# Attention scores beside the values' column tile, copies by quarters, and one finishing chain for two heads

## The chip, the cores and the metric

The kernel runs on one core of a Trainium2 chip. The metric is the time of one execution in microseconds on the device, and the profile shown below is of one execution on that core. The engines are TensorE (PE: matmuls; PEld: its weight loads), VectorE (DVE), ScalarE (ACT), GpSimd (POOL, here mostly an issuer of DMAs) and SyncE (SP, which issues the weight loads).

## The reference

The reference is one encoder layer over two sequences of 256 tokens with 2048 features, all in float32:

```python
h = h + W_out [ NA(heads 0..7) ; GatedDeltaNet-bidir(heads 0..7) ]( RMSNorm(h) )
h = h + SwiGLU( RMSNorm(h) )
y = RMSNorm(h)
```

`NA` is neighbourhood attention on a grid of 64 columns: per head, scores q k^T plus a position bias, a softmax over the allowed window, and a product with v. `GatedDeltaNet-bidir` runs, for each head, a convolution over q, k and v, and then a recurrence over four chunks of 64 tokens in both directions. Each chunk needs the inverse of a unit triangular 64x64 matrix; there are 128 of them (2 directions, 4 chunks, 8 heads, 2 sequences), one for each partition. The result of a head is normalised by its root mean square and multiplied by a gate silu(z). Both groups go through one output projection, and a feed-forward block follows.

## The kernel before, in words

Every large product is split in three: a float32 operand is written as hi + lo, and `mm3` runs hi*hi, hi*lo and lo*hi. The weights arrive by DMA on SP's queue, ScalarE writes hi (`split`, line 134), VectorE writes lo (line 135), and three buffers of each are in flight. Outputs are made in column tiles of 128 features by 512 tokens (`col_tile`). A column tile is two half tiles (`half_gemm`), each with 24 matmuls of 512 columns.

Small work is put between the matmuls by generators. `half_gemm` calls `pump()` after every second k, so four times in a half tile; I call this a step. `pump` advances the first generator of the queue `chains` and the first of the queue `side`, each to its next `yield`. At the end of a half tile it advances `vector_work` once. `pause(n)` yields n times. So a constant such as `NA_START = 8` says how many steps, each a quarter of a half tile, lie between two pieces of a chain.

TensorE's instructions are pinned to the order of the program: `mm` and `transpose` go through `pin`. On the other engines a planner orders the instructions at compile time by its own estimate of when each is ready. `pin` keeps an instruction behind the one that the program issued before it on the same engine; the copies of `kkq` (line 484) and the first operation of `norms` (line 490) are pinned in that way. Every engine then runs its list strictly in order.

The stages around the change are these. First come the K and Q column tiles of the eight recurrent heads; `kq_post` stores each head's Gram matrices to DRAM (`s_gram`). When the last is stored, the generator `lanes` is put into `vector_work`. It gathers the matrices back with one matrix on each partition (`kkq`, four DMAs by quarters), copies each quarter from the lower to the upper half of the partitions on ScalarE, scales them, solves the triangular systems on VectorE (the loop with `prod` and `W`, lines 557 and 559, 156 instructions of each kind), and stores the result to DRAM (`s_uq`, line 573).

Meanwhile TensorE runs the attention column tiles: for each of eight heads Q, K and V, six half tiles, numbered here from 0 for the first half of head 0's Q. After V, `attend(h)` is put into `chains`. It loads the bias, waits `NA_START` steps, transposes V and makes the scores (lines 605 and 611); the softmax runs on VectorE and ScalarE (lines 619 to 628). `NA_GAP` steps later it transposes the probabilities (line 635), and `PV_GAP` steps later it makes the output product, which `na_o` (line 647) copies and line 648 stores. A head takes 24 steps, so chain and column tiles keep pace.

Then come two column tiles for each recurrent head, its v and its gate z. `prepare` loads the solved matrices (`uq`, line 690, by POOL) and k and q of a head. `recur_pair` runs the four chunks of two heads in step, the first product being `dvn` with `uq` (line 747). `finish_head` squares the output (line 798, written to the tile `yo`, which has one buffer, shared with `pT`), makes a reciprocal square root by Newton steps on VectorE, scales the output `os` (line 806), transposes it (line 812), multiplies by the gate and splits the result into `dmix` (lines 137 and 138). `yo` holds that product too until the split. PSUM has three banks for small products (`sm_tile`) and three for column tiles.

Of the kernel before, what the change touches and what calls it, by code (L numbers as in the profile page):

```python
# [8 lines left out]
F32 = mybir.dt.float32  # L9
# [3 lines left out]
AF = mybir.ActivationFunctionType  # L13
ALU = mybir.AluOpType
# [4 lines left out]
P = 128  # L19
T = 512  # L20
# [3 lines left out]
NB = 2  # L24
# [16 lines left out]


AHEAD = 120
NA_START = 8
NA_GAP = 10
PV_GAP = 5
KQ_START = 20
KQ_GAP = 8
CORE_START = 2
S_GAP = 3  # L50
R_GAP = 2
LANE_START = 4

EARLY = 3
N_GAP = 2
# [10 lines left out]
def r32(ap):  # L66
    return ap.bitcast(F32)
# [3 lines left out]
def hybrid_encoder(ctx: ExitStack, tc: tile.TileContext, xT, w_in, w_ba, w_out, w_gate,  # L71
                   w_up, w_down, w_group, nw_mix, nw_ffn, nw_fin, na_bias, conv_w, lane_par,
                   dn_nw, y):
    nc = tc.nc
    act = nc.scalar.activation
    tt = nc.vector.tensor_tensor
# [5 lines left out]
    def mm(*a, **k):  # L82
        pin(nc.tensor.matmul(*a, **k))  # L83

    def transpose(*a):
        pin(nc.tensor.transpose(*a))
# [16 lines left out]
    ident = cons.tile([P, P], F32, name="ident")  # L103
# [13 lines left out]
    dnw = cons.tile([P, 1], F32, name="dnw")  # L117
# [13 lines left out]
    def split(hi, lo, src, scale=None):  # L131

        if scale is None:
            act(out=hi, in_=src, func=AF.Copy)  # L134
            tt(lo, src, r32(hi), ALU.subtract)  # L135
        else:
            act(out=hi, in_=src, func=AF.Copy, scale=scale)
            stt(lo, src, scale, r32(hi), ALU.mult, ALU.subtract)
# [27 lines left out]
    chains = []  # L166
    side = []
# [24 lines left out]
    def pause(n):  # L192
        for _ in range(n):
            yield
# [11 lines left out]
    def col_tile(src, xs):  # L206
        ps = pg.tile([P, T], F32, tag="g", name="ps_g")
        half_gemm(ps, src[0], xs[:8], True, False)
        half_gemm(ps, src[1], xs[8:], False, True)
        return ps  # L210
# [20 lines left out]
    def sm_tile():  # L231
        return psm.tile([P, T], F32, tag="s", name="ps_s")
# [20 lines left out]
    ps = sm_tile()  # L253
# [46 lines left out]
    def evac(ps, tag, bufs=1, pool=None):  # L300
        t = (pool or wk).tile([P, T], F32, tag=tag, bufs=bufs, name="ev_" + tag)
        pin(tt(t, ps, rstd, ALU.mult))
        return t
# [27 lines left out]
    def ranged(ap, pp):  # L331

        a = ap.rearrange("p (b c t) -> p b c t", b=NB, c=4)
        return a[:, :, 0:4:3] if pp == 0 else a[:, :, 1:3]
# [19 lines left out]
    na = na_cm.__enter__()  # L354
# [40 lines left out]
    rqs = wk.tile([P, 2, 16], F32, tag="rqs", name="rqs")  # L395
# [76 lines left out]
    def lanes():  # L472
# [7 lines left out]
        for d in range(2):  # L480
            nc.gpsimd.dma_start(qq[half[d]], s_qq.rearrange("k h b t -> (k h b) t"))
        yield from pause(LANE_START)
        for sl in quarters:
            pin(nc.scalar.copy(kkq[half[1], sl], kkq[half[0], sl]))
        yield


        def norms(src, nm):
# [41 lines left out]
        ps = sm_tile()  # L530
        mm(ps[:, :P], ones, dg, start=True, stop=True)
        nc.scalar.copy(egl, ps[:, :P])
        ps = sm_tile()
# [5 lines left out]
        for hf in range(2):  # L539
            for pp in range(2):  # L540
                l0 = 3 * P + POS[pp][hf] * 16
# [9 lines left out]
        for c in range(1, C):  # L551
            for s0 in range(0, c, BLK):
# [3 lines left out]
                pv = pr[:, :n * j].rearrange("p (s j) -> p s j", j=j)  # L556
# [20 lines left out]
    for h in range(H):  # L577
# [3 lines left out]
        ps = (ps_k0, ps_k1)[h] if h < 2 else col_tile(w_in[2 * h], xs)  # L581
        conv_silu(ps, 8 + h, kq[:, 0])
        ps = ps_q0 if h == 0 else col_tile(w_in[2 * h + 1], xs)
# [12 lines left out]
        chains.append(kq_post(h, kq, sqh, sql))  # L596


    def attend(h, qT, kT, vT):
        bias = na.tile([P, 2, L], F32, tag="bias", bufs=2, name="bias")  # L600
        nc.gpsimd.dma_start(bias, na_bias[h])
        yield from pause(NA_START)
        pv = sm_tile()
        for i in range(4):
            transpose(pv[:, i * P:i * P + P], vT[:, i * P:i * P + P], ident)
        pq = []
        for b in range(NB):
            ps = sm_tile()
            pq.append(ps)
            for qi in range(2):  # L610
                mm(ps[:, qi * L:qi * L + L], qT[:, b * L + qi * P:b * L + qi * P + P],
                   kT[:, b * L:b * L + L], start=True, stop=True)
        vn = na.tile([P, 4, P], F32, tag="vn", name="vn")
        nc.scalar.copy(vn, pv.rearrange("p (i d) -> p i d", i=4))
        sc = []
        for b in range(NB):
            s = na.tile([P, 2, L], F32, tag=f"s{b}", name="na_s")
            sc.append(s)
            tt(s, pq[b].rearrange("p (q k) -> p q k", q=2), bias, ALU.add)
            mx = na.tile([P, 2], F32, tag="mx", bufs=2, name="mx")  # L620
            nc.vector.tensor_reduce(mx, s, AX.X, ALU.max, negate=True)
            sm = na.tile([P, 2], F32, tag="sm", bufs=2, name="sm")
            for qi in range(2):
                act(out=s[:, qi], in_=s[:, qi], func=AF.Exp, bias=mx[:, qi:qi + 1],
                    accum_out=sm[:, qi:qi + 1])
            nc.vector.reciprocal(sm, sm)
            for qi in range(2):
                act(out=s[:, qi], in_=s[:, qi], func=AF.Copy, scale=sm[:, qi:qi + 1])
        yield from pause(NA_GAP)
        pT = []  # L630
        for b in range(NB):
            pt = sm_tile()
            for kt in range(2):
                for qi in range(2):
                    transpose(pt[:, kt * L + qi * P:kt * L + qi * P + P],
                              sc[b][:, qi, kt * P:kt * P + P], ident)
            t = na.tile([P, 2, L], F32, tag=("pT", "pU")[b], name="pT")
            nc.scalar.copy(t, pt.rearrange("p (q k) -> p q k", q=2))
            pT.append(t)
        yield from pause(PV_GAP)  # L640
        no = na.tile([P, T], F32, tag="s0", name="na_o")
        po = sm_tile()
        for b in range(NB):
            for kt in range(2):
                mm(po[:, b * L:b * L + L], vn[:, b * 2 + kt], pT[b][:, kt],
                   start=(kt == 0), stop=(kt == 1))
        nc.scalar.copy(no, po)
        nc.gpsimd.dma_start(s_na[h], no)

    for h in range(H):  # L650
        ps = col_tile(w_in[16 + 3 * h], xs)
        qT = na.tile([P, T], F32, tag="qT", name="qT")
        pin(stt(qT, ps, QSCALE, rstd, ALU.mult, ALU.mult))
        ps = col_tile(w_in[16 + 3 * h + 1], xs)
        kT = evac(ps, "kT", 1, na)
        ps = col_tile(w_in[16 + 3 * h + 2], xs)
        vT = evac(ps, "vT", 1, na)
        chains.append(attend(h, qT, kT, vT))


    dr_cm = tc.tile_pool(name="dr", bufs=1, side="right", reuse_waits="tile")
# [16 lines left out]
    prepared, outputs, gate, traced, finished = {}, {}, {}, set(), set()  # L678
# [101 lines left out]
    def recur_pair(h):  # L780
        while not {h, h + 1} <= set(prepared):
            yield
        yield from pause(CORE_START)
        yield from together(recur(h), recur(h + 1))
        for i in (h, h + 1):
            side.append(finish_head(i))

    def finish_head(h):
        dr, dmix = state["dr"], state["dmix"]
        while h not in gate:  # L790
            yield
        zs, os_ = gate[h], outputs[h]

        ssq = dr.tile([P, 2, NB], F32, tag="ssq", bufs=2, name="ssq")
        yo = na.tile([P, T], F32, tag="pT", name="yo")
        for pp in (1, 0):
            for b in range(NB):
                act(out=yo[:, :P], in_=os_[:, pp, b], func=AF.Square,
                    scale=rqs[:, pp, h * NB + b:h * NB + b + 1], accum_out=ssq[:, pp, b:b + 1])
        yield  # L800
        rs = dr.tile([P, 2, NB], F32, tag="rs", bufs=2, name="rs_o")
        ts(ssq, ssq, 1.0 / P, EPS, ALU.mult, ALU.add)
        newton_rsqrt(rs, ssq, dr)
        tt(ssq, rs, rqs[:, :, h * NB:h * NB + NB], ALU.mult)
        for pp in (1, 0):
            tt(os_[:, pp], os_[:, pp], ssq[:, pp, :, None].broadcast_to([P, NB, P]), ALU.mult)
        yield from pause(FIN_GAP)
        po = sm_tile()
        po4 = po.rearrange("p (b q t) -> p b q t", b=NB, q=2)
        for pp in range(2):  # L810
            for b in range(NB):
                transpose(po4[:, b, pp], os_[:, pp, b], ident)
        for pp in range(2):
            tt(ranged(yo, pp), po4[:, :, pp].rearrange("p b (c t) -> p b c t", c=2),
               ranged(zs, pp), ALU.mult)
        split(dmix[:, 0, h], dmix[:, 1, h], yo, dnw)
        finished.add(h)

    def start_waiting():
        open_recurrence()  # L820
# [5 lines left out]
    for h in range(0, H, 2):  # L826
        vT = []
        for i in range(2):
# [5 lines left out]
            ps = col_tile(w_in[40 + 2 * (h + i)], xs)  # L834
# [4 lines left out]
        for i in range(h, h + 2):  # L839
            ps = col_tile(w_in[40 + 2 * i + 1], xs)  # L840
            while i > 3 and i - 4 not in finished:
                pump()
            zs = evac(ps, ("vn", "s0", "pU", "zs")[i % 4], 1, state["dr"] if i % 4 == 3 else na)
# [16 lines left out]
    dmix = state["dmix"]  # L860
# [4 lines left out]
    for i in pairs:  # L865
        ps = pg.tile([P, T], F32, tag="g", name="ps_g")
# [7 lines left out]
    for i in pairs[:EARLY]:  # L874
        ps = pg.tile([P, T], F32, tag="g", name="ps_g")
# [30 lines left out]
    for n, i in enumerate(pairs):  # L906
# [3 lines left out]
        else:  # L910
            hk = st.tile([P, T], F32, tag="hk", bufs=2, name="hk")
            nc.sync.dma_start(hk, s_h1[i])
            if n < EARLY:
                ps, wh, wl = early[n]
                mm3(ps, wh[:, 7], wl[:, 7], dns[7][0], dns[7][1], False, True)
            else:
                ps = pg.tile([P, T], F32, tag="g", name="ps_g")
# [418 lines left out]
```

## Time and profile before

| what | value |
|---|---|
| median of 3 runs | 2306.1 us (2305.64 to 2307.92) |
| the profiled execution | 2303.48 us, its span 2301.7 us |
| TensorE busy | 2265.5 us, 98% of the span |
| VectorE busy | 1773.7 us, 77% |
| ScalarE busy | 1067.7 us, 46% |
| mean granted clock of TensorE | 0.994 |

A row of a group or a timeline names the engine, the line of the kernel, the operation, and output and inputs by the program's names, with x for the number of instructions. Many instructions have the line of a helper: 83 is the body of `mm`, 86 that of `transpose`, 134, 135, 137 and 138 those of `split`. The text in brackets is the engine's idle time just before, and what ended it. The times of the timeline are microseconds from the start of the span.

### The profile page before, as it was taken

How to read it: one execution, taken by the hardware profiler on the slowest of the kernel's cores; microseconds unless marked ns; L12 is line 12 of the kernel's file. 1: busy time of each engine (PE TensorE's matmuls, PEld its weight loads, DVE VectorE, ACT ScalarE, POOL GpSimd, SP SyncE). 2: the span in 40 equal slices, each digit the busy share in tenths (PEclk: the TensorE clock that was granted, in tenths of full speed). 3: DMA queues.
4: the chain of work that ended last, by engine and by line, in shares of the span. 5: the costliest groups of instructions: out<-in, count | busy, mean ns of one | idle time of the engine just before them, and what ended most of it. 6: DMA issues, size and time to landing. Idle time of an engine off the chain costs nothing.

```text
span 2301.7 us, 32536 instructions
## 1 busy us (share of the span) xinstructions
PE 2265.5 (98%) x12318; PEld 1928.6 (84%) x12318; DVE 1773.7 (77%) x2740; ACT 1067.7 (46%) x1642; POOL 242.8 (11%) x342
## 2 busy tenths in 40 slices
PE   9999999999999999999999999999999999999998
PEld 6887787888877888788888888888888878888887
DVE  7754699984564645888888888888888778889866
ACT  6777323234332424644444444444444464444435
POOL 2211100002000110100111001101000011011110
PEclk9999999999999999999999999999999999999999
DMA  5333422246331654677777777777776477667772
GB/s 205 126 129 131 122 92 96 97 128 147 102 104 62 215 160 160 207 202 200 211 200 203 195 207 199 207 198 209 196 193 181 153 212 198 176 181 216 183 198 87
DMA packets 112573, 384.74 MB, mean 167 GB/s; under 512 B 14080, under 2 KB 14416, under 8 KB 112160
## 3 DMA queue, kind: packets, MB, share of 16 engines
q1 hardware_dynamic: 77264, 267.17, 33.6%
q0 software_dynamic: 35152, 115.49, 23.7%
q8 instruction: 97, 1.59, 0.3%
q14 instruction: 60, 0.49, 0.1%
HBM read 347.20 MB, written 35.41 MB: 166 GB/s over the span
## 4 chain that ended last, share of the span: by engine, by line
PE 80%; DVE 9%; ACT 5%; issue 3%; DMA 3%; POOL 0%; SPq 0%; DVEq 0%; ACTq 0%; POOLq 0%
PE ps_g L83 25%; PE ps_a L83 14%; PE ps_d L83 14%; PE ps_c L83 14%; PE ps_b L83 7%; PE ps_s L83 5%; DVE w_lo L135 2%; DVE cacc L346 1%; ACT w_hi L134 1%; DVE W L559 1%; DVE prod L557 1%; ACT E L467 1%; PE ps_o L83 1%; DMA w_first<-in_w_group_dram 1%; ACT E L469 1%
## 5 line engine op out<-in xcount | busy, mean ns | idle before, releaser
L83 PE MATMUL ps_g<-xhi,w_hi 128*128 128x512 f32 x896 | 360.9, 403 | 1.9 <-DVE on L437 1.4
L83 PE MATMUL ps_g<-xhi,w_lo 128*128 128x512 f32 x896 | 352.0, 393 | 2.5 <-DVE w_lo L135 2.5
L83 PE MATMUL ps_g<-xlo,w_hi 128*128 128x512 f32 x896 | 351.7, 392 | 0.9 <-DVE xlo L250 0.9
L134 ACT ACTIVATE w_hi<-w_first 128x1024 fp32r<-128x1024 f32 (+1 forms) x180 | 185.7, 1032 | 287.0 <-PE ps_c L83 160.6
L135 DVE TENSOR_TENSOR w_lo<-w_raw,w_hi 128x1024 fp32r<-128x1024 f32 x166 | 202.5, 1221 | 138.5 <-ACT w_hi L134 134.8
L134 ACT ACTIVATE w_hi<-w_raw 128x1024 fp32r<-128x1024 f32 x166 | 174.8, 1055 | 255.9 <-PE ps_g L83 220.8
L134 ACT ACTIVATE w_hi<-b 128x1024 fp32r<-128x1024 f32 (+1 forms) x180 | 185.7, 1031 | 227.3 <-issue 121.9
L135 DVE TENSOR_TENSOR w_lo<-w_first,w_hi 128x1024 fp32r<-128x1024 f32 (+1 forms) x180 | 213.6, 1186 | 52.6 <-ACT w_hi L134 48.1
L135 DVE TENSOR_TENSOR w_lo<-b,w_hi 128x1024 fp32r<-128x1024 f32 (+1 forms) x180 | 212.8, 1182 | 3.0 <-ACT w_hi L134 2.8
L83 PEld LDWEIGHTS ps_g<-xhi,w_lo 128*128 128x128 f32 x896 | 169.5, 189 | 39.9 <-DVE w_lo L135 3.9
L83 PEld LDWEIGHTS ps_g<-xhi,w_hi 128*128 128x128 f32 x896 | 169.8, 189 | 39.6 <-issue 4.4
L83 PEld LDWEIGHTS ps_g<-xlo,w_hi 128*128 128x128 f32 x896 | 169.8, 189 | 36.9 <-DVE xlo L250 2.6
L83 PE MATMUL ps_a<-xc,w_hi 128*128 128x512 f32 x704 | 176.3, 392 | 2.2 <-DVE p L959 2.2
L83 PE MATMUL ps_d<-xc,w_hi 128*128 128x512 f32 x704 | 176.3, 392 | 0.0
L83 PE MATMUL ps_c<-xc,w_hi 128*128 128x512 f32 x704 | 176.3, 392 | 0.0
L83 PEld LDWEIGHTS ps_a<-xc,w_hi 128*128 128x128 f32 x704 | 126.7, 189 | 25.7 <-issue 3.0
L83 PEld LDWEIGHTS ps_d<-xc,w_hi 128*128 128x128 f32 x704 | 126.6, 189 | 22.6
L83 PEld LDWEIGHTS ps_c<-xc,w_hi 128*128 128x128 f32 x704 | 126.6, 189 | 22.6
L134 ACT ACTIVATE w_hi<-w_second 128x1024 fp32r<-128x1024 f32 (+1 forms) x60 | 61.9, 1032 | 92.6 <-PE ps_d L83 84.3
L83 PEld LDWEIGHTS ps_a<-xc,w_lo 128*128 128x128 f32 x704 | 96.0, 190 | 6.9
L83 PEld LDWEIGHTS ps_c<-xc,w_lo 128*128 128x128 f32 x704 | 96.0, 190 | 6.9
L83 PEld LDWEIGHTS ps_d<-xc,w_lo 128*128 128x128 f32 x704 | 96.0, 190 | 6.9
(362 smaller groups left out, 4258.8 us busy)
## 6 DMA issues: line engine op xcount, KB each, us to landing
w_raw<-in_w_in_dram SPq DMA_DIRECT2D x110, 512.0 KB, 3.3
b<-in_w_gate_dram SPq DMA_DIRECT2D x66, 512.0 KB, 3.9
b<-in_w_up_dram SPq DMA_DIRECT2D x66, 512.0 KB, 4.5
b<-in_w_group_dram SPq DMA_DIRECT2D x48, 448.0 KB, 4.1
w_raw<-in_w_out_dram SPq DMA_DIRECT2D x32, 512.0 KB, 3.5
w_raw<-in_w_down_dram SPq DMA_DIRECT2D x24, 512.0 KB, 3.7
w_second<-in_w_gate_dram SPq DMA_DIRECT2D x22, 512.0 KB, 5.7
w_first<-in_w_gate_dram SPq DMA_DIRECT2D x22, 512.0 KB, 5.0
```

What stands on the lines that cost most here:

```text
L83: pin(nc.tensor.matmul(*a, **k))
L134: act(out=hi, in_=src, func=AF.Copy)
L135: tt(lo, src, r32(hi), ALU.subtract)
L346: stt(a3[:, :, lo:hi], x3[:, :, lo + o:hi + o], cw[:, ct, j:j + 1], a3[:, :, lo:hi], ALU.mult, ALU.add)
L467: pin(act(out=E[half[0], s, s:], in_=G[half[0], s:], func=AF.Exp, bias=NG[half[0], s:s + 1]))
L469: pin(act(out=E[half[1], s, :s + 1], in_=G[half[1], :s + 1], func=AF.Exp, bias=NG[half[1], s:s + 1]))
L557: tt(pv, W[:, s0:s1, s0:c], kkq[:, c, 0, None, s0:c].broadcast_to([P, n, j]), ALU.mult)
L559: nc.vector.tensor_reduce(W[:, s0:s1, c], pv, AX.X, ALU.add)
```

## The change

There are three parts.

1. `attend` gets V in a list that is filled later. It is put into `chains` after K's column tile, so that its first steps lie beside V's column tile. The scores come `NA_START = 5` steps after that (formerly 8 steps after V). The transposes of V and the copy `vn` move from ahead of the scores to just ahead of the transposes of the probabilities, `NA_GAP = 13` steps (formerly 10) behind the scores. A loop yields there until V is in the list.
2. In `lanes` the `yield` moves into the loop over the quarters, so one copy is issued at the end of each of four half tiles instead of four at the end of one, and `LANE_START` goes from 4 to 6. All that follows in `lanes` is issued five half tiles later in the program.
3. `finish_pair` takes the place of two `finish_head`, one behind the other. It squares the outputs of both heads, runs the Newton steps once on a tile of twice the size, scales both, and `FIN_GAP` steps later transposes both into two PSUM banks, multiplies and splits them one after the other. The wait for the gate moves from its start to ahead of the transposes.

```diff
-NA_START = 8
-NA_GAP = 10
+NA_START = 5
+NA_GAP = 13
...
-LANE_START = 4
+LANE_START = 6
...
         for sl in quarters:
             pin(nc.scalar.copy(kkq[half[1], sl], kkq[half[0], sl]))
-        yield
+            yield
...
-    def attend(h, qT, kT, vT):
+    def attend(h, qT, kT, v):
         bias = na.tile([P, 2, L], F32, tag="bias", bufs=2, name="bias")
         nc.gpsimd.dma_start(bias, na_bias[h])
         yield from pause(NA_START)
-        pv = sm_tile()
-        for i in range(4):
-            transpose(pv[:, i * P:i * P + P], vT[:, i * P:i * P + P], ident)
...
-        vn = na.tile([P, 4, P], F32, tag="vn", name="vn")
-        nc.scalar.copy(vn, pv.rearrange("p (i d) -> p i d", i=4))
...
         yield from pause(NA_GAP)
+        while not v:
+            yield
+        pv = sm_tile()
+        for i in range(4):
+            transpose(pv[:, i * P:i * P + P], v[0][:, i * P:i * P + P], ident)
+        vn = na.tile([P, 4, P], F32, tag="vn", name="vn")
+        nc.scalar.copy(vn, pv.rearrange("p (i d) -> p i d", i=4))
...
         kT = evac(ps, "kT", 1, na)
+        v = []
+        chains.append(attend(h, qT, kT, v))
         ps = col_tile(w_in[16 + 3 * h + 2], xs)
-        vT = evac(ps, "vT", 1, na)
-        chains.append(attend(h, qT, kT, vT))
+        v.append(evac(ps, "vT", 1, na))
...
-        for i in (h, h + 1):
-            side.append(finish_head(i))
+        side.append(finish_pair(h))
+
+    def finish_pair(h):
+        dr, dmix = state["dr"], state["dmix"]
+        ssq = dr.tile([P, 2, 2, NB], F32, tag="ssq", bufs=2, name="ssq")
+        yo = na.tile([P, T], F32, tag="pT", name="yo")
+        for i in range(2):
+            for pp in (1, 0):
+                for b in range(NB):
+                    l0 = (h + i) * NB + b
+                    act(out=yo[:, :P], in_=outputs[h + i][:, pp, b], func=AF.Square,
+                        scale=rqs[:, pp, l0:l0 + 1], accum_out=ssq[:, i, pp, b:b + 1])
         yield
+        rs = dr.tile([P, 2, 2, NB], F32, tag="rs", bufs=2, name="rs_o")
         ts(ssq, ssq, 1.0 / P, EPS, ALU.mult, ALU.add)
         newton_rsqrt(rs, ssq, dr)
+        tt(ssq, rs, rqs[:, :, h * NB:(h + 2) * NB].rearrange("p q (i b) -> p i q b", i=2),
+           ALU.mult)
+        for i in range(2):
+            for pp in (1, 0):
+                os_ = outputs[h + i]
+                tt(os_[:, pp], os_[:, pp], ssq[:, i, pp, :, None].broadcast_to([P, NB, P]),
+                   ALU.mult)
         yield from pause(FIN_GAP)
+        while h + 1 not in gate:
+            yield
+        pos = []
+        for i in range(2):
+            po = sm_tile().rearrange("p (b q t) -> p b q t", b=NB, q=2)
+            for pp in range(2):
+                for b in range(NB):
+                    transpose(po[:, b, pp], outputs[h + i][:, pp, b], ident)
+            pos.append(po)
+        for i in range(2):
+            if i:
+                yo = na.tile([P, T], F32, tag="pT", name="yo")
+            for pp in range(2):
+                tt(ranged(yo, pp), pos[i][:, :, pp].rearrange("p b (c t) -> p b c t", c=2),
+                   ranged(gate[h + i], pp), ALU.mult)
+            split(dmix[:, 0, h + i], dmix[:, 1, h + i], yo, dnw)
+            finished.add(h + i)
```

More of the change, by code (lines that the diff above doesn't have):

```diff
@@ L784, in recur_pair @@
         yield from together(recur(h), recur(h + 1))
-        for i in (h, h + 1):
-            side.append(finish_head(i))
-    def finish_head(h):
+        side.append(finish_pair(h))
+    def finish_pair(h):
         dr, dmix = state["dr"], state["dmix"]
[L790 to L794, printed above, removed]
+        ssq = dr.tile([P, 2, 2, NB], F32, tag="ssq", bufs=2, name="ssq")
         yo = na.tile([P, T], F32, tag="pT", name="yo")
[L796 to L799, printed above, removed]
+        for i in range(2):
[4 more added lines that the diff above has]
+                        scale=rqs[:, pp, l0:l0 + 1], accum_out=ssq[:, i, pp, b:b + 1])
@@ L800, in finish_head @@
         yield
-        rs = dr.tile([P, 2, NB], F32, tag="rs", bufs=2, name="rs_o")
+        rs = dr.tile([P, 2, 2, NB], F32, tag="rs", bufs=2, name="rs_o")
         ts(ssq, ssq, 1.0 / P, EPS, ALU.mult, ALU.add)
         newton_rsqrt(rs, ssq, dr)
-        tt(ssq, rs, rqs[:, :, h * NB:h * NB + NB], ALU.mult)
-        for pp in (1, 0):
-            tt(os_[:, pp], os_[:, pp], ssq[:, pp, :, None].broadcast_to([P, NB, P]), ALU.mult)
-        yield from pause(FIN_GAP)
-        po = sm_tile()
-        po4 = po.rearrange("p (b q t) -> p b q t", b=NB, q=2)
@@ L810, in finish_head @@
[L810 to L817, printed above, removed]
+        tt(ssq, rs, rqs[:, :, h * NB:(h + 2) * NB].rearrange("p q (i b) -> p i q b", i=2),
[5 more added lines that the diff above has]
+                   ALU.mult)
```

## The prediction

> **What bounds the kernel now.** I read the page first, then the waits of TensorE, then the timelines of the engines named there.
>
> ```profile
> span 2301.7 us, 32536 instructions
> ...
> PE 2265.5 (98%) x12318; PEld 1928.6 (84%) x12318; DVE 1773.7 (77%) x2740; ACT 1067.7 (46%) x1642; POOL 242.8 (11%) x342
> ```
>
> TensorE is busy for 2265.5 of 2301.7 us, and the change gives it the same matmuls and transposes as before. It can win only what TensorE idles, and what idling does to its clock. So the waits of PE are the view that matters (columns: total us, times, longest):
>
> ```profile
> PE ps_s L86 <- DVE os L806: 4.4, 2, 3.8
> ...
> PE ps_s L86 <- ACT na_s L628: 3.7, 3, 1.6
> PE ps_g L83 <- DVE w_lo L135: 3.3, 3, 2.0
> ...
> PE ps_g L83 <- ACT w_hi L134: 0.4, 1, 0.4
> ```
>
> Each is next to one part of the change: the finish of a head (L806), the softmax ahead of the transposes of the scores (L628), and the split of a weight tile (L134, L135). For the last, the timelines of ScalarE and of VectorE:
>
> ```profile
> 238.78 1.91 ACT L484 COPY kkq<-kkq 64x2048 f32<-64x2048 f32 x1 [9.71 <-DMA kkq<-s_gram]
> ...
> 243.81 1.06 ACT L134 ACTIVATE w_hi<-w_raw 128x1024 fp32r<-128x1024 f32 x1
> ...
> 248.53 1.90 ACT L484 COPY kkq<-kkq 64x2048 f32<-64x2048 f32 x1 [0.99 <-DMA kkq<-s_gram]
> ```
>
> ```profile
> 244.90 1.23 DVE L135 TENSOR_TENSOR w_lo<-w_raw,w_hi 128x1024 fp32r<-128x1024 f32 x1 [10.13 <-ACT w_hi L134]
> ...
> 250.46 0.22 DVE L490 TENSOR_SCALAR nkx<-kkq 128x64 f32<-128x64 f32 x1 [3.73 <-ACT kkq L484]
> ...
> 282.46 0.15 DVE L557 TENSOR_TENSOR prod<-W,kkq 128x1 f32<-128x1 f32 x1
> ```
>
> ScalarE stands in order behind copies whose data are still landing (9.71 us), the weight split at 243.81 stands behind two of them, and VectorE loses 10.13 and 3.73 us. VectorE has no time to lose, since it then runs the triangular solve (L557, L559) beside everything else:
>
> ```profile
> 253.90:257.40 3.50, 3.10 (x9) 2.57 (x10) 3.50 (x4) 0.14 (x1) 0.00 (x0) 0.51 0.46 150
> 315.40:318.80 3.40, 3.40 (x13) 2.91 (x12) 3.40 (x8) 2.66 (x12) 0.00 (x0) 0.50 0.44 154
> 356.30:359.80 3.50, 3.50 (x11) 2.85 (x12) 3.50 (x6) 2.36 (x4) 0.00 (x0) 0.51 0.38 138
> 690.80:697.70 6.90, 5.37 (x15) 4.43 (x16) 3.35 (x9) 1.35 (x2) 0.00 (x0) 0.51 0.10 39
> 420.00:460.00 40.00, 40.00 (x185) 33.31 (x184) 40.00 (x64) 12.30 (x22) 1.08 (x2) 1.00 0.26 93
> ```
>
> These are stretches with length, then PE, PEld, DVE, ACT and POOL busy, then the granted clock. From 420 to 460 us VectorE is busy for 40.00 of 40.00 us. The first four rows are the second price of the stalls: beside them the clock fell to 0.51, so 17.3 us ran at half speed.
>
> **Part 1, scores and copies: what goes.** The output copy of each attention head, one per 24 steps (a step is a quarter of a half tile), gives the pace:
>
> ```profile
> 283.73 0.59 ACT L647 COPY na_o<-ps_s 128x512 f32<-128x512 f32 x1 [0.91 <-PE ps_s L83]
> ...
> 325.65 0.59 ACT L647 COPY na_o<-ps_s 128x512 f32<-128x512 f32 x1 [0.91 <-PE ps_s L83]
> ...
> 366.97 0.59 ACT L647 COPY na_o<-ps_s 128x512 f32<-128x512 f32 x1 [0.91 <-PE ps_s L83]
> ...
> 404.51 0.59 ACT L647 COPY na_o<-ps_s 128x512 f32<-128x512 f32 x1 [0.90 <-PE ps_s L83]
> ```
>
> The heads take 41.9, 41.3 and 37.5 us; the last is undisturbed, 1.56 us a step. Two heads are 8.2 us too long, of which I leave 1 us to the transposes of the lanes, which come once: 7.2.
>
> ```profile
> 896.71 0.50 PE L83 MATMUL ps_g<-dmix,w_lo 128*128 128x512 f32 x1 [0.79 <-DVE w_lo L135]
> ```
>
> Before the first copy lie 3.3 + 0.4 us of weight waits, less 0.8 that belongs to a much later stage (this row), one softmax wait of about 1.1, and half of 3.5 us of low clock less 0.4 counted already: 5.3. Together 12.5 us.
>
> The new code spreads the four copies over four half tiles, starting two later: by a count of steps they stand behind the splits of half tiles 8 to 11, when the data have landed. Then neither ScalarE nor VectorE blocks, and the gap of 13 steps instead of 10 gives the softmax 4.7 us more, three times its longest wait. I take all 12.5; the bounds are 7.4 (3.7 + 3.7, the idle alone) and 13.7.
>
> On the clock the Trainium skill (TensorE: Matmul & The Clock Gate, "HAM oscillation") says that idle gaps above about 3.4 us make it fall. The trace differs: the longest softmax wait is 1.6 us, and the clock fell beside two of three. By that rule only the idle goes, the finish below would give 2.7 us less, and the sum would be 2.7 us higher. I take the trace.
>
> **Part 1, what it moves.** The evacuation of K is followed by the scores 6 steps (9.4 us) later, formerly 17. The bias load and the store of the head before keep their order on POOL's queue. The wait for the values' tile adds nothing: it is written 8 steps after the chain starts and read 18 steps after. Transposes of V keep their number and only change place. All this I cost at nothing, because TensorE has column tiles in between; without that cover the evacuation of K is the risk (a rival below).
>
> What is not free is the solve. The fourth copy now stands in program order behind the softmax of head 1, which is issued in the sixth step of its V tile. Before, the end of that tile was at 281.8 us (2 us ahead of the copy at 283.73). Two steps earlier, less 5.3 of stalls, plus 1.9 for the output product now ahead: about 275.5. The scores take 2; the softmax its length in this trace:
>
> ```profile
> 267.23 0.67 DVE L619 TENSOR_TENSOR na_s<-ps_s,bias 128x512 f32<-128x512 f32 x1
> ```
>
> ```profile
> 273.64 0.91 ACT L628 ACTIVATE na_s<-na_s,sm 128x256 f32<-128x256 f32 x2 [0.73 <-DVE sm L626]
> ```
>
> That is 7.3, less 1 that overlaps the scores, and a copy is 1.9: the copies end at 284 to 286 instead of 250.4. From there to the solve it took 32.0 us of VectorE (250.46 to 282.46). Half of that needs only the first three copies and can run ahead, so I take 16: the solve starts near 301, 18 us later. The bounds are 286 (all ahead) and 317 (nothing ahead). It ends later by as much, since VectorE has no gap to catch up in, and a little more because it now shares with more attention work: 20 us.
>
> **Part 1, who waits for that.** The solve's result goes through DRAM to the recurrence:
>
> ```profile
> 493.75 2.28 DVE L567 TENSOR_TENSOR kkq<-W,rb 64x2048 f32<-64x2048 f32 x1
> ...
> 497.80 3.85 DVE L569 TENSOR_TENSOR kkq<-W,nks 64x2048 f32<-64x2048 f32 x1
> ```
>
> ```profile
> 496.33 1.56 POOL L573 DMA_DIRECT2D s_uq<-kkq  x2 [15.33 <-DVE kkq L567]
> 501.95 0.77 POOL L573 DMA_DIRECT2D s_uq<-kkq  x1 [4.06 <-DVE kkq L569]
> 518.05 0.57 POOL L648 DMA_DIRECT2D s_na<-na_o  x1 [15.33 <-ACT na_o L647]
> ...
> 544.87 4.73 POOL L690 DMA_DIRECT2D uq<-s_uq  x7 [16.17 <-DMA s_uq<-kkq]
> ```
>
> ```profile
> 560.06 1.05 PE L83 MATMUL ps_s<-dvn,uq 128*128 128x128 f32 x8
> ```
>
> ```profile
> DMA to landing us min/median/max: 2.9/4.3/17.0
> ```
>
> The last load is issued at 549.6 and lands 4.3 later, at 553.9; the first product needs it at 560.1. So there are 6 us in hand. The change spends them three times. TensorE comes 12.5 us sooner. The recurrence itself is placed three steps sooner (4.7 us): the attention chain of head 7 now ends a column tile earlier and the new pair is first in the queue. So the need is at 560.1 - 12.5 - 4.7 = 542.9. The data come 20 us later, less what POOL's queue gives back: it stood 15.33 us behind the store of head 6, which is a column tile earlier now. The stores still land one after the other, so I take 11 of it: 553.9 + 20 - 11 = 563. The bounds are 547 (solve not moved, 7 given back) and 574 (nothing given back).
>
> TensorE then waits 563 - 542.9 = 20.1 us with the whole program queued behind the product, since its order is fixed. After such an idle the clock is low. At 690.8 a 3.78 us idle left 5.4 us of half speed behind it, worth 2.7; I take 2.6.
>
> **Part 2, the finish in pairs.**
>
> ```profile
> 685.17 0.40 ACT L798 ACTIVATE yo<-os,rqs 128x128 f32<-128x128 f32 x1 [0.82 <-DVE dmix L138]
> ```
>
> ```profile
> 692.33 1.09 PE L86 MATMUL ps_s<-ident,os 128*128 128x128 f32 x4 [3.78 <-DVE os L806]
> ...
> 834.94 0.63 PE L86 MATMUL ps_s<-ident,os 128*128 128x128 f32 x4 [0.64 <-DVE os L806]
> ```
>
> The squares of a second head waited until the first head's result had left the shared buffer yo (L138); the transposes then came too soon. One chain takes the squares of both at once, so 3.78 + 0.64 and the 2.7 of low clock go: 7.1 us. The four squares (0.40 each) and two scalings (0.4) added to each chain lie ahead of transposes 6 steps away, and these steps are short where no recurrence runs beside them. I put 1 us for new waits, bounds 0 and 4. The thirteen small VectorE operations saved per pair save nothing here: no PE wait stands behind them any more. The wait for the gate never holds, since the gates are written at least five half tiles sooner.
>
> **Sum, on the profiled execution.** -12.5 + 20.1 + 2.6 - 7.1 + 1.0 = +4.1 us. That execution took 2303.5 us (span 2301.7 and 1.8 around it), 2.6 under the median of the runs, 2306.1. I carry the difference to the median and round up, as more of the unknown bounds point up: 2311.
>
> **Rivals.**
>
> The data are there in time. If the work ahead of the solve fits before the last copy, or the planner sets the copies sooner, the loads land by 547: 16 us less than the forecast, 2294 or so, and at best, with no wait at all, -12.5 - 7.1 = 2286. It decides from a solve that starts before about 285. For it: VectorE would not lose 13.9 us in front of the solve. Against it: the copy is kept behind the softmax by the program order. Chance 0.28.
>
> K comes too late. With the scores 6 steps behind K, an evacuation more than 9.4 us late stops TensorE. The last matmuls of K, and its evacuation, for heads 1 and 4:
>
> ```profile
> 268.25 0.39 PE L83 MATMUL ps_g<-xhi,w_lo 128*128 128x512 f32 x1
> ...
> 390.54 0.39 PE L83 MATMUL ps_g<-xhi,w_lo 128*128 128x512 f32 x1
> ```
>
> ```profile
> 279.81 0.69 DVE L302 TENSOR_TENSOR ev_kT<-ps_g,rstd 128x512 f32<-128x512 f32 x1
> ...
> 395.65 0.67 DVE L302 TENSOR_TENSOR ev_kT<-ps_g,rstd 128x512 f32<-128x512 f32 x1
> ```
>
> The lag is 11 us in the disturbed head and 5 in the other. If it persists: some 3 us and a clock drop of 1.7 in each of three heads; much of it would shorten the wait at the recurrence. Or the finish holds two of three PSUM banks while the next pair steps: up to 4 a pair. Either adds 8 to 15 us: 2319 to 2326. Chance 0.14.
>
> The copies do not move because the planner, not the yields, sets the order: then the 12.5 stay, the recurrence needs its data at 555 when they land at 554, and the finish gives 7: 2300. Chance 0.06.
>
> The clock rule of the Trainium skill above would give 2314; it lies inside the forecast.
>
> **Numbers.** Forecast (the wait at the recurrence eats the gain, -2 to +14): chance 0.52, of which 0.20 within 0.2% and 0.32 slower. About 0.2%, 4.6 us, is what a measurement of this kernel can tell from no change. Faster: 0.28 + 0.04 = 0.32; same 0.20 + 0.02 = 0.22; slower 0.32 + 0.14 = 0.46. The range 2290 to 2322 leaves out the best of the first rival and the worst of the second.
>
> **What would show it.** Right: no copy of kkq with a DMA wait, no PE wait on na_s or os above 0.5 us, head copies 37.5 us apart from the start, the first L557 near 300, and one PE wait of 10 to 25 us on uq near 545. Wrong: the first product of the recurrence without a wait (the faster rival), or PE waiting for ev_kT (the slower).

## The result, and the profile after

The changed kernel is slower: 2322.6 us (median of 6 runs, 2321.2 to 2323.5) against 2305.3 us for the kernel before beside it (6 runs, 2302.4 to 2307.9). The ratio is 1.0075, with a 95% interval of 1.0062 to 1.0088, so the loss is 17.3 us. The forecast, 2311 us, was 11.6 us too low, and the range ended at 2322, just short of it.

The page of the changed kernel, its span and its first row of busy times:

```profile
span 2321.2 us, 32510 instructions
...
PE 2265.6 (98%) x12318; PEld 1930.8 (83%) x12318; DVE 1762.3 (76%) x2688; ACT 1065.8 (46%) x1640; POOL 242.7 (10%) x342
```

TensorE is busy as long as before (2265.6 against 2265.5 us). Its idle time, span less busy, grew from 36.2 to 55.6 us. That is 19.4 of the 19.5 us between the two spans, so in the net the loss is idle time, and the waits of PE must show it (total us, times, longest):

```profile
PE ps_s L83 <- DMA uq<-s_uq: 21.9, 4, 20.1
PE ps_s L86 <- ACT dvT L350: 9.4, 3, 8.2
PE ps_c L83 <- ACT w_hi L134: 5.2, 2, 3.2
...
PE ps_g L83 <- DVE w_lo L135: 0.8, 1, 0.8
...
PE ps_s L86 <- DVE os L811: 0.3, 1, 0.3
```

The two rows on top are new. Before, `uq` cost no wait in the list and `dvT` 0.7 us. The waits that the change was to remove are gone: none on `na_s`, 0.3 us on `os` (4.4 before), 0.8 us on `w_lo` (3.3 before). The net of the listed rows is 21.9 + 8.7 + 1.1 - 3.7 - 4.1 - 2.5 = +21.4 us; the other listed rows bring it to 19.9, and idle that the view does not list to 19.4.

The timeline of PE has the two long waits, each in the bracket at the end of its row:

```profile
543.41 1.21 PE L86 MATMUL ps_s<-ident,dvT 128*128 128x128 f32 x4 [8.22 <-ACT dvT L350]
...
571.41 0.77 PE L83 MATMUL ps_s<-dvn,uq 128*128 128x128 f32 x2 [20.10 <-DMA uq<-s_uq]
```

The first is the transposes of a recurrent head's V, the second the first product of the recurrence. To see why both came late, follow the solve backwards. These are the copies on ScalarE, and then VectorE from the fourth copy to the end of the solve:

```profile
252.14 1.91 ACT L484 COPY kkq<-kkq 64x2048 f32<-64x2048 f32 x1
...
257.40 1.90 ACT L484 COPY kkq<-kkq 64x2048 f32<-64x2048 f32 x1
...
265.88 1.90 ACT L484 COPY kkq<-kkq 64x2048 f32<-64x2048 f32 x1
...
281.37 1.90 ACT L484 COPY kkq<-kkq 64x2048 f32<-64x2048 f32 x1
```

```profile
283.31 0.22 DVE L490 TENSOR_SCALAR nkx<-kkq 128x64 f32<-128x64 f32 x1 [2.32 <-ACT kkq L484]
283.77 2.28 DVE L517 TENSOR_TENSOR kkq<-kkq,E 128x2048 f32<-128x2048 f32 x1
...
312.34 0.16 DVE L557 TENSOR_TENSOR prod<-W,kkq 128x1 f32<-128x1 f32 x1
...
532.91 3.72 DVE L569 TENSOR_TENSOR kkq<-W,nks 64x2048 f32<-64x2048 f32 x1
536.67 1.23 DVE L135 TENSOR_TENSOR w_lo<-w_raw,w_hi 128x1024 fp32r<-128x1024 f32 x1
537.81 0.68 DVE L302 TENSOR_TENSOR ev_xi<-ps_g,rstd 128x512 f32<-128x512 f32 x1
```

No copy waits for a DMA any more (the longest such wait before was 9.71 us), and VectorE waits 2.32 us for the last copy where it lost 10.13 and 3.73 us. But the fourth copy ends at 283.3 (250.4 before), and not one scaling of `kkq` lies ahead of it: the first, line 517, is at 283.77, behind the read of the diagonal, line 490. The solve starts at 312.3 (282.5 before) and its last operation ends at 536.6 (501.7 before). Behind it in VectorE's order stands the evacuation `ev_xi` of a column tile whose last matmul ended at 527.1. From it come `dvT` on ScalarE (542.94) and the 8.22 us of TensorE.

The result then goes through DRAM, on POOL's queue:

```profile
533.17 1.56 POOL L573 DMA_DIRECT2D s_uq<-kkq  x2 [40.49 <-DVE kkq L567]
...
543.01 0.57 POOL L651 DMA_DIRECT2D s_na<-na_o  x1
...
568.31 4.73 POOL L694 DMA_DIRECT2D uq<-s_uq  x7 [8.89 <-DMA s_uq<-kkq]
```

The stores land one after the other from 541.2 to 567.7, and the loads from 568.7 to 575.4.

### The profile page after: what moved, and what is told of

Read it like the earlier page. It is cut to its first block, busy times and chain, and to the rows that moved or that the text cites. A ratio compares the mean times of both kernels' runs of the same rounds, so it can differ in the third digit from the quotient of the medians.

```text
span 2321.2 us, 32510 instructions
## 1 busy us (share of the span) xinstructions
PE 2265.6 (98%) x12318; PEld 1930.8 (83%) x12318; DVE 1762.3 (76%) x2688; ACT 1065.8 (46%) x1640; POOL 242.7 (10%) x342
## 4 chain that ended last, share of the span: by engine, by line
PE 78%; DVE 12%; ACT 4%; issue 3%; DMA 3%; POOL 0%; SPq 0%; DVEq 0%; ACTq 0%; POOLq 0%
PE ps_g L83 23%; PE ps_a L83 14%; PE ps_c L83 14%; PE ps_d L83 14%; PE ps_b L83 7%; PE ps_s L83 5%; DVE w_lo L135 3%; DVE prod L557 3%; DVE W L559 2%; DVE cacc L346 1%; DMA s_uq<-kkq 1%; ACT w_hi L134 1%; PE ps_o L83 1%; ACT E L467 1%; ACT E L469 1%
```

## The experiments

Three kernels make one part of the change each, beside runs of the kernel before at 2304.7 us. First the copies by quarters alone:

```diff
-LANE_START = 4
+LANE_START = 6
...
-        yield
+            yield
```

> The kernel before with part 2 alone (LANE_START 6, a yield behind each of the four copies). Theory A, the copies carry the loss: the solve starts about 30 us later than in the kernel before (282.5), near 312; the loads of uq land near 573 and the first product of the recurrence, due near 553, waits some 15 to 20 us; slower than before by 6 to 14 us. Rival B, the earlier place of the recurrence (attention chain a column tile sooner) carries it: here the recurrence keeps its place, so no wait on uq above 6 us, and the kernel is faster by 5 us or more because the weight splits are no longer blocked. Rival C, the pairs carry it: as B.

Measured: 2312.4 us, ratio 1.0030 (1.0020 to 1.0040), 7.7 us slower. Its waits of PE:

```profile
PE ps_s L86 <- ACT na_s L628: 6.8, 2, 5.8
...
PE ps_s L86 <- DVE os L806: 4.4, 2, 3.8
PE ps_s L83 <- DMA uq<-s_uq: 4.3, 4, 2.5
```

The solve starts at 308.9, and the last load of `uq` lands at 566.0 instead of 554.1. Yet the wait on it is only 4.3 us, where theory A had 15 to 20: TensorE is ready for the transposes of the last attention head 14.5 us sooner than before (530.5 against 545.0), but waits 5.8 us there for the softmax, behind the late solve, and with further waits and the low clock behind them it asks for `uq` at 559.5, as late as the kernel before (560.1). So the late solve alone costs something, but not what it costs in the whole change.

Then the attention scores alone:

```diff
-NA_START = 8
-NA_GAP = 10
+NA_START = 5
+NA_GAP = 13
...
+        chains.append(attend(h, qT, kT, v))
         ps = col_tile(w_in[16 + 3 * h + 2], xs)
```

> The kernel before with part 1 alone (the attention chain starts beside V's column tile, V is transposed late). Theory A: the solve starts near 282 as before; the recurrence comes three steps sooner, but the store of head 6 no longer stands in POOL's queue, so its loads land near 545 and no wait on uq exceeds 4 us; the softmax waits (3.7 us) go, the blocked weight split stays; between 6 us faster and the same. Rival B: the wait on uq is there (8 us or more) and the kernel is slower by 5 us or more. Another possibility: PE waits for the evacuation of K, 3 us in each of heads 1 to 3.

Measured: 2302.9 us, 0.9991 (0.9982 to 1.0001). The softmax waits are gone, but `uq` is waited for, 3.4 us, the longest 2.3. The solve starts at 279.2.

And the finish in pairs alone:

```diff
-        for i in (h, h + 1):
-            side.append(finish_head(i))
+        side.append(finish_pair(h))
```

> The kernel before with part 3 alone (finish_pair). Theory A: the wait of 3.8 us on os at head 3, its low clock (2.7 us) and the 0.6 us wait at head 7 go, new waits are under 1 us; faster by 4 to 7 us. Rival C, the pairs carry the loss (two of three PSUM banks held, yo handed on within the chain): PE waits of 2 us or more per pair, slower by 3 us or more.

Measured: 2299.0 us, 0.9975 (0.9966 to 0.9985), 5.7 us faster. No wait on `os` of 0.2 us or more is left. This part does about what it was costed at (7.1 less 1.0).

The three effects add up to 7.7 - 1.8 - 5.7 = +0.2 us; together the parts cost 17.3. So the loss lies in how they meet, and the next kernel takes out the part that is late, and keeps the other two:

```diff
-LANE_START = 6
+LANE_START = 4
...
-            yield
+        yield
```

> The changed kernel with part 2 undone (LANE_START 4, all four copies at the end of one half tile). Theory A: ScalarE blocks on the gather again and the weight split waits as before, but the solve starts near 282, the loads of uq land by 548, the wait on uq is under 6 us: faster than before by 6 to 14 us. Rival B: the wait on uq stays above 12 us and the kernel stays slower than before by 8 us or more.

Measured: 2297.9 us, 0.9970 (0.9958 to 0.9982). Two of its waits:

```profile
PE ps_s L83 <- DMA uq<-s_uq: 2.9, 2, 2.4
...
PE ps_s L86 <- ACT dvT L350: 1.1, 2, 0.6
```

Both new waits of the changed kernel have nearly gone, with the solve at 278.3 and the last load landed at 552.2. On top of parts 1 and 3, the copies by quarters cost 1.0075 - 0.9970 of 2305 us, 24 us.

Is it the lateness that costs, or the moving of the copies itself? One kernel keeps the quarters and starts them four half tiles sooner; another keeps the lateness and lets the recurrence ask 12 steps later.

```diff
-LANE_START = 6
+LANE_START = 2
```

> The changed kernel with LANE_START 2 instead of 6, the yields between the copies kept: the copies now stand behind half tiles 4 to 7. Theory A (what costs is how late the last copy stands in the order, not that the copies are spread): the solve starts near 280, the loads of uq land by 554, the wait on uq is under 5 us; faster than before by 6 to 12 us. Rival D (the spreading itself, one copy between the weight splits of each half tile, costs): a wait on uq of 10 us or more stays, slower than before.

Measured: 2305.8 us, 1.0005 (0.9996 to 1.0014). Its waits:

```profile
PE ps_s L86 <- DVE na_s L615: 5.2, 1, 5.2
...
PE ps_s L83 <- DVE ev_kT L302: 2.6, 1, 2.6
PE ps_s L83 <- DMA uq<-s_uq: 2.5, 2, 1.9
```

The solve starts at 286.2 and the wait on `uq` is down from 21.9 to 2.5 us. So the lateness carried that wait. But the 6 to 12 us of theory A did not come, the time is that of the kernel before, and the gain is smaller than that of the kernel with the copies as before: VectorE now scales beside the second head's K, whose evacuation stands behind the scaling of 275.13 (line 525), and TensorE waits for it at 277.67. The 5.2 us come at 327.07, where transposes wait until VectorE has read the scores (line 615). The former is the rival "K too late" of the prediction, at one head and behind the scaling. These waits are not the whole difference: of the 9.1 us between the spans of the two kernels (2304.8 and 2295.7) 3.2 are idle and 5.9 busy time, and this execution has 13.6 us of half speed from 977 us on, in stages without copies, where the other has none before the end of the program.

```diff
-CORE_START = 2
+CORE_START = 14
```

> The changed kernel with CORE_START 14 instead of 2, so the recurrence of each pair is issued 12 steps (some 16 us of column tiles) later. Theory A: the solve and the loads keep their times (312, 575), the wait on uq falls from 20 us to 8 or less, the low clock behind it shrinks, the wait of 8 us on the transposes of V stays; 10 to 18 us faster than the changed kernel, so within 8 us of before. Rival E (the recurrences are the path that sets the end, so what is moved comes back as a wait in the finish of the last pairs): less than 5 us faster than the changed kernel.

Measured: 2306.1 us, 1.0005 (0.9996 to 1.0015), 16 us less than the changed kernel.

```profile
PE ps_s L83 <- DMA uq<-s_uq: 9.8, 4, 8.0
PE ps_s L86 <- ACT dvT L350: 8.3, 1, 8.3
```

The solve is as late as in the changed kernel (313.0), the data even land later (579.7), and nearly all of the loss is gone: twelve more steps of column tiles now lie ahead of the need. So it is the meeting of late data with an early need that costs, and the two waits are of different kinds: the one on `uq` shrank by 12 us, the one on `dvT`, which lies ahead of the recurrence, stayed.

Next the step of the prediction that said that half of the scaling could run ahead of the fourth copy. The diagonal (line 490) is read by quarters, each behind its copy:

```diff
         for sl in quarters:
             pin(nc.scalar.copy(kkq[half[1], sl], kkq[half[0], sl]))
+            pin(ts(nkx[:, sl], dgk[:, sl], EPS, None, ALU.add))
             yield
```

> The changed kernel, in which the diagonal of the gathered matrices is read by quarters, each right behind its copy, instead of once behind the last. If the read of the diagonal keeps back all scaling of the gathered matrices (lines 517 to 527) until the fourth copy has landed, then three quarters of it now run ahead, the solve starts near 300 instead of 312, the loads of uq land 8 to 12 us earlier (565) and the kernel is faster than the changed one by 8 to 12 us. If the scaling is held by something else (the planner's order, the copies themselves), the solve stays within 3 us of 312 and the time within 4 us.

Measured: 2317.0 us, 1.0052 (1.0037 to 1.0067), 5.5 us less than the changed kernel by the medians, short of the 8 to 12 expected, and the ends of the intervals overlap. The trace is of the fastest of its four runs (2312.4 us). VectorE, where lines 487, 522, 530 and 562 answer to 490, 517, 525 and 557, and two waits of PE:

```profile
254.97 1.55 DVE L530 TENSOR_TENSOR kkq<-kkq,E 64x768 f32<-64x768 f32 x1
...
269.12 2.28 DVE L522 TENSOR_TENSOR kkq<-kkq,E 128x2048 f32<-128x2048 f32 x1
...
283.92 0.17 DVE L487 TENSOR_SCALAR nkx<-kkq 128x16 f32<-128x16 f32 x1 [2.91 <-ACT kkq L486]
...
304.97 0.16 DVE L562 TENSOR_TENSOR prod<-W,kkq 128x1 f32<-128x1 f32 x1
```

```profile
PE ps_s L83 <- DMA uq<-s_uq: 20.2, 4, 18.1
...
PE ps_s L86 <- ACT dvT L350: 3.3, 3, 2.1
```

Now the first scaling, 254.97, runs 29 us ahead of the end of the fourth copy (283.9), and the first of line 522 (269.12) 15 us ahead; the solve starts 7.4 us sooner, and the last load lands 8.8 us sooner (566.6). So the whole-tile read of the diagonal did hold them back. It is not all: 16 us were counted, and 21 us still lie between the last copy and the solve. The scalings that now run ahead take 7.6 us together. Behind the fourth copy stay those that need its quarter, the Newton steps, which are made once from the whole diagonal, and the four products with `ndm` (line 532), which need their result. The wait on `dvT` shrinks with the solve's end (6 us), and that on `uq` only by 1.7 in total, since the need came sooner by nearly as much as the data.

The last three kernels look for a better version: the early copies with the recurrence at its old place, three steps later (the scores' earlier chain had moved it three sooner); the same with the copies as before; and the diagonal by quarters with a middle start.

```diff
-CORE_START = 2
+CORE_START = 5
...
-LANE_START = 6
+LANE_START = 2
```

> The changed kernel with LANE_START 2 and CORE_START 5: the copies as early as in the run with LANE_START 2, and the recurrence three steps (4 us) later, where it was in the kernel before. Theory A: no wait on uq, none on the weight splits, none on the softmax; 10 to 16 us faster than the kernel before. Rival: a wait remains, no better than LANE_START 2 alone.

Measured: 2296.7 us, 0.9970 (0.9959 to 0.9982), 9 us less than with the early copies alone, and 8 us less than the kernel before, short of the 10 to 16 expected. No wait on `uq` is listed, but 5.6 us on `na_s` (line 615) and 3.2 us on `ev_kT` remain.

```diff
-CORE_START = 2
+CORE_START = 5
...
-LANE_START = 6
+LANE_START = 4
...
-            yield
+        yield
```

> Parts 1 and 3 with the copies as before (all four at once, LANE_START 4), and CORE_START 5. In the run of parts 1 and 3 alone the wait on uq was 2.9 us, with 6.8 us of low clock beside it. Theory A: three steps more (4 us) take both away; 4 to 6 us faster than parts 1 and 3 alone, so 10 to 13 us faster than before. Rival: the wait moves to the transposes of V or the finish, within 2 us of parts 1 and 3 alone.

Measured: 2290.0 us beside 2306.5 before, 0.9929 (0.9915 to 0.9942). It is the fastest of all, 16 us ahead of the kernel before. From its page, and its first product of the recurrence:

```profile
span 2288.4 us, 32509 instructions
...
PE 2257.7 (99%) x12318; PEld 1924.5 (84%) x12318; DVE 1764.6 (77%) x2688; ACT 1064.0 (46%) x1640; POOL 242.0 (11%) x342
```

```profile
552.53 1.05 PE L83 MATMUL ps_s<-dvn,uq 128*128 128x128 f32 x8
```

The product has no wait in its bracket, and its last load landed at 551.7. Against the same kernel without the three steps the median is 7.9 us lower, more than the wait of 2.9 us that went: the idle fell by 2.1 us (32.8 to 30.7) and the busy time by 5.2 (2262.9 to 2257.7), with the mean granted clock at 0.998 instead of 0.995. Ahead of the end of the program the kernel without the three steps ran 3.4 us from 294.9 and 6.8 us from 550.9, beside the wait on `uq`, at half speed, the one with them only 3.4 us from 1864.5. This is one profiled execution of each.

```diff
-CORE_START = 2
+CORE_START = 5
...
-LANE_START = 6
+LANE_START = 3
...
             pin(nc.scalar.copy(kkq[half[1], sl], kkq[half[0], sl]))
+            pin(ts(nkx[:, sl], dgk[:, sl], EPS, None, ALU.add))
             yield
```

> The changed kernel with the diagonal read by quarters, LANE_START 3 and CORE_START 5: copies behind half tiles 5 to 8, scaling spread behind each copy. Theory A: no blocked weight split, no heap of VectorE work in front of head 1's softmax as with LANE_START 2, solve from 275 to 285, no wait on uq; 12 to 16 us faster than before. If the heap comes back (a wait of 5 us on na_s or ev_kT in heads 1 and 2), 6 to 9 us faster.

Measured: 2292.9 us, 0.9946 (0.9933 to 0.9958). The interval overlaps that of the fastest, so which of the two is better stays open. The solve starts at 287.7, later than the 275 to 285 expected, and one wait of 3.9 us stands at 536.04, on the copy of the last head's probabilities; the trace is of the slowest of the five runs. What matters to both is that the data are there before they are asked for.

## Why the prediction was wrong

The sign of the sum and the place of its largest term were right, and the size was not: +4.1 us were worked out, and the spans of the two profiled executions differ by 19.5 (the medians by 17.3). Two steps failed: that half of the scaling could run ahead of the fourth copy, and that column tiles would cover every other evacuation, for which the sum had nothing. Behind the second lie 11.5 of the 15.4 us that the sum missed, and the first made it worse.

**Stalls ahead of the recurrence, -12.5: held.** The copies of the heads' outputs come at an even pace:

```profile
265.27 0.59 ACT L650 COPY na_o<-ps_s 128x512 f32<-128x512 f32 x1 [0.91 <-PE ps_s L83]
...
302.81 0.59 ACT L650 COPY na_o<-ps_s 128x512 f32<-128x512 f32 x1 [0.91 <-PE ps_s L83]
...
378.60 0.59 ACT L650 COPY na_o<-ps_s 128x512 f32<-128x512 f32 x1 [0.91 <-PE ps_s L83]
```

The first three distances sum to 113.3 us instead of 120.8, a gain of 7.5 where 7.2 was counted. TensorE begins half tile 52, the last to start ahead of the wait on `dvT`, at 528.4 instead of 540.9 us, 12.5 sooner, and by then it has made the last head's transposes and product too, which before came behind this point (about 2.4 us). The gain is nearer 15.

**The finish, -7.1 + 1.0: held.** The kernel with the pairs alone gains 5.7 us, and in the changed kernel the only wait on `os` is 0.3 us.

**"Half of that ... can run ahead": this step failed.** The solve was put at 301, with 317 as the bound for nothing ahead, and it started at 312.3. The copies ended where they were put (283.3, forecast 284 to 286). The read of the diagonal needs all four quarters, and the scalings of lines 525 to 527 write over what it reads, so each had to follow it. Line 517 writes the other half of the tile and yet came behind it too; whether the whole tile is guarded there or the planner chose this order, no run separates. The diagonal by quarters shows the effect: with that read split, both kinds run ahead, 7.6 us of work, and 7.4 us come back, less than half of the 16 that were counted. I had looked at which quarters the scaling needs, and not at which reads must be done before it may write.

From there the data were late by 35.0 us at the solve's end (536.6 against 501.7), where 20 was counted: 29.9 in the start and 5.1 in a longer solve. The queue gave back 13.7 (52.5 us from the solve's end to the last load before, 38.8 after) instead of 11. So the last load landed at 575.4, not 563.

**The wait on `uq`, 20.1: right by two errors.** It measured 20.10 us. The data came 12.4 us later than forecast, but the product starts when the second of the eight loads is in, at 571.3, and not the last. And the need, forecast for 542.9, came at 551.3 (571.4 less 20.1), because the wait on `dvT` stood ahead of it. That the two cancel is luck.

**The wait on `dvT`: not in the sum at all, and the largest term missed.** "TensorE has column tiles in between" was said of the attention's evacuations. The same VectorE has to evacuate the recurrent heads' V, and its order places that behind the solve's last three long operations. A solve that ends late there takes TensorE with it: 8.22 us, 8.7 more than before in all. The kernel with the diagonal by quarters, whose solve ends 9.9 us sooner (526.7), brings the longest down to 2.1, and the one with the copies as before to 0.6.

**The low clock, +2.6 after the wait, was too small.** The stretches at half speed: length, then PE, PEld, DVE, ACT and POOL busy, then the granted clock:

```profile
543.40:549.00 5.60, 5.59 (x17) 4.69 (x18) 2.01 (x4) 0.85 (x2) 3.82 (x5) 0.50 0.98 191
571.40:579.80 8.40, 6.55 (x17) 4.99 (x18) 0.88 (x2) 1.96 (x4) 1.65 (x3) 0.50 0.26 70
996.20:999.60 3.40, 3.40 (x14) 3.01 (x13) 0.13 (x1) 1.26 (x2) 0.00 (x0) 0.50 0.92 330
1897.30:1900.70 3.40, 2.84 (x7) 2.26 (x8) 1.09 (x1) 1.30 (x2) 0.62 (x1) 0.50 1.09 216
```

Half of the busy time in each is lost: 2.8 + 3.3 + 1.7 + 1.4 = 9.2 us. (One more at the end of each program, with PE busy for 1.19 us in it, is the same in both.) The second row is the term that was costed at 2.6. The first belongs to the wait that was not forecast. The last two lie behind waits of 2.16 and 3.16 us in late stages that the change does not touch. With the same working the four stretches shown of before cost 7.7, so the changed kernel spent nearly as much time at half speed as the one before, in other places, and busy time hardly moved.

**The account.** Forecast +4.1; to it 8.7 of idle on `dvT` and 2.8 of slow clock behind it; 0.7 more of slow clock and 1.8 of smaller waits on `uq`; 3.1 of slow clock and 1.1 of wait (`ps_c`) in the late stages; 2.4 more gain ahead of the recurrence and 0.7 fewer waits in the finish. That gives 4.1 + 11.5 + 2.5 + 4.2 - 3.1 = 19.2 of the 19.5 us. The wait on `uq` itself needs no correction, since its two errors cancel. The 4.2 us of the late stages belong to this execution; nothing here ties them to the change.

On the rule that I weighed, the Trainium skill (TensorE: Matmul & The Clock Gate, "HAM oscillation") puts the danger at idle gaps above about 3.4 us. Here 8.22 and 20.10 us brought the clock down, as it says, but so did the stretch behind 2.16 us at 995, while the same idle in the same place before did not:

```profile
994.97 2.69 PE L83 MATMUL ps_a<-xc,w_hi 128*128 128x512 f32 x8 [2.16 <-DVE p L972]
```

```profile
978.63 2.08 PE L83 MATMUL ps_a<-xc,w_hi 128*128 128x512 f32 x8 [2.16 <-DVE p L959]
```

The first row is of after, the second of before: eight matmuls in 2.69 us or in 2.08. What differs is where the idle lies. Within each of the twelve traces the granted clock falls at times that are whole multiples of 3.413 us apart. After, one such stretch runs from 992.8 to 996.2, the idle (992.81 to 994.97) lies wholly in it, and the clock fell at its end; before, an edge at 977.6 divides the idle (976.48 to 978.63). All twelve traces have this idle of 2.16 us, and in the five in which it lies within one stretch the clock fell, in the seven in which an edge divides it, it did not. So the length of a gap alone does not say whether it will cost.

The prediction also priced that rule of the Trainium skill wrongly: the idle of 3.78 us ahead of the finish is longer than 3.4, so by the rule its 2.7 us would have stayed in the gain. What would have gone is the low clock beside the shorter waits, 12.5 - 7.4 = 5.1 us at most.

**The rivals.** "The data are there in time" did not come; its condition, a solve before about 285, is met in the kernel with the copies as before (278.3, 2297.9 us against the 2294 that the rival gave). Having the data in time, with the recurrence three steps later, gave 2290.0. "K too late" did not show in the changed kernel, whose listed waits have no `ev_kT`; it did at one head with the early copies. The other half of that rival, a finish that holds the PSUM banks, did not come either: the pairs alone are faster. And the copies did move, the last from 248.5 to 281.4, so the planner did not undo the yields.

## What to carry to other kernels

Before you say that a step can run ahead of a late input, look at its writes as well as its reads: here one early read of the whole tile kept back every write in place until the last part was there. When a long chain on a busy engine is moved back, list everything that stands behind its end in that engine's order, and not only the consumer of its result; here an evacuation with no part in the solve cost 8 us. And when one part of a change makes the need earlier and another the data later, cost them together: alone these parts came to +0.2 us, together to +17.3, and moving the need three steps back made the first and third part worth 16 us.

## What the runs showed of the hardware

The clock fell 3.6 and 4.6 us after TensorE began to idle (538.8 and 555.9, the idle starting at 535.2 and 551.3) and came back only 5.6 and 8.4 us after matmuls resumed. The Trainium skill (TensorE: Matmul & The Clock Gate, "What's actually happening") gives about 3.4 us for the fall and about 3.4 us of sustained work for the return. Counted from the first idle moment and from the first matmul, the fall agrees roughly and the return was slower.

The times of the changes themselves say why. In this trace the clock changed at 538.8, 549.0, 555.9, 579.8, 996.2, 999.6, 1897.3 and 1900.7 us, and the distances are 3, 2, 7, 122, 1, 263 and 1 times 3.413 us. So in this trace it changes only at the edges of stretches of that length, wherever TensorE's idle begins. The stretches from 535.4 to 538.8 and from 552.5 to 555.9 were the first without any work. The one from 542.2 to 545.6 had PE busy for 2.22 us of it, and only the next, to 549.0, for all of it; behind the second idle the first that was busy throughout is the one from 576.4 to 579.8. Counted in these stretches, one without work ended the full clock, and one of unbroken work brought it back. The one from 992.8 ended it too, with PE busy for 1.24 us, so where the limit between them lies is not shown.
